# A hybrid encoder layer on one core: the order of loads at attention's opening, the place of the row maxima, and the step at which the output projection begins

## The chip, the cores and the metric

One core of a Trainium2 chip runs the whole program. The metric is the device time of one execution in microseconds; the figure for a kernel is the median of its runs. Engines are named as in the profile: PE is TensorE's matmul, PEld its weight load, ACT is ScalarE, DVE is VectorE, POOL is GpSimd, SP is SyncE, which here only issues DMAs.

## The reference, cut to what matters

One layer on 2048 tokens of width 1024, in float32:

```python
proj = jnp.einsum('btd,de->bte', x, w_in[l])
q, k, v, u, vs = jnp.split(proj, splits, axis=-1)     # 512 columns each
a_out = neighbourhood_attention(q, k, v, na_rel_bias[l])
s_out = spatial_gating(jax.nn.gelu(u), jax.nn.gelu(vs), ...)
mixed = jnp.concatenate([rms_norm(a_out, ...), rms_norm(s_out, ...)], axis=-1)
mix_out = jnp.einsum('bte,ed->btd', mixed, w_out[l])
x = layer_norm(DEEPNORM_ALPHA * x + mix_out, ln1_g[l], ln1_b[l])
moe_out = hierarchical_moe(x, ...)                    # 16 experts, two for each token
x = layer_norm(DEEPNORM_ALPHA * x + moe_out, ln2_g[l], ln2_b[l])
```

Attention has 8 heads of 64. The tokens form a grid of 32 rows of 64, and each attends to a window of 8 by 16 neighbours.

## The kernel before, in words

**Precision.** Each float32 factor is split into a high and a low part (`split`, line 142: ACT casts the high part, line 143; DVE subtracts it to give the low part, line 144), and each product is three matmuls (`passes`, lines 133 to 135). A "k step" of one 128-row block is thus three matmuls of up to 512 columns.

**Stage A, the input projection** (`phase_a`, line 147). Tokens come in two halves, columns in five groups of 512: Q (0), K (1), V (2), U (3), VS (4). One call of `block` does one column group of one half: two sets of four accumulators, and for each set eight k steps. While it runs, it loads the next group's eight weight pieces (`load_w`, 256 KB each: four at the first four k steps of either set). A piece goes through one of three raw buffers `wr`, is cast by ACT two turns later and finished by DVE. At the end of each set a `fin_...` function evicts the accumulators. For K (`fin_k`, line 362) that is an ACT cast and a DVE subtraction for each of the four, into staging tiles `mt` and `kt`, and four stores into the DRAM tensor `kd`.

The last call is `block(1, 1, ..., 2, then=attn_open(...))`: K of the second half, while the V weights are loaded. The V projection of that half isn't done in stage A. It is `late_v` (line 445), a generator over eight units of 128 tokens that does four k steps at each call; it serves as PE's filler in the first attention steps.

**Attention's opening** (`attn_open`, line 504) is a generator that `block` advances once for each k step of its second set. At its first call it closes the pools `sp` and `ev` and opens pool `ai` in their place, clears the `qb` and `lg` tiles on DVE, and loads K, Q and bias of group 0. The following calls load V block 0, then K, Q and bias of group 1, then V block 1, then the other two biases. A V block (`load_v`) is 256 tokens in four column pieces, each loaded by four DMAs of 48 or 64 KB: 16 DMAs.

**Attention** (`phase_b`, line 565). 128 steps, from a loop `for i in range(n + 5)`. Step i computes the scores of piece i (PE, three matmuls into a bank of tag `l`), adds the bias and takes the row maximum (DVE, line 644, into `lg` and `m`); it does the exponent of step i - 1 (ACT, line 651), the reciprocal of its sum (DVE, 656) and its scaling (POOL, 657); it transposes the probabilities of step i - 3 (PE, 670; ACT copies them into `pT`, 672). Odd steps mix steps i - 5 and i - 4 with V (PE, line 686). Tiles `m`, `s`, `pT` and the outputs of even groups come from pool `at`, which is opened on the same side as `ai` once stage A's pools are closed, and so takes over memory that stage A's staging tiles had; a tile waits for the last user of the memory that it gets.

What fills PE between scores: `late_v` in steps 0 to 13, nothing in steps 14 to PSTART - 1, then `project` (line 898), the output projection with 16 units of 128 tokens and eight turns each, one turn a step. A turn has six matmuls of 512 columns on average. After the loop the turns that are left run by themselves, with the first loads of the expert stage between them. Unit u needs the attention output of its 256 tokens; that of units 0 and 1 is complete after step 19. After a unit's last turn, `after` (line 719) does the layer norm and the routing in later turns: statistics, then POOL's root (line 728), then two DVE operations (730, 731), then PE's transposes of the normed rows (741), each a turn apart. In the loop, PSTART also places the first load of `sr` (step PSTART - 5), the first load of residual rows (PSTART) and four parameter loads (PSTART + 2). The split of the output weights (`load_wo`, lines 611 to 624) runs on ACT and DVE in steps 14 to 21.

**The expert stage** (`Moe`) follows: gathers, gate, up and down products of 16 experts with their weights streamed from HBM, and the last layer norm.

**Order.** PE, ACT, DVE and POOL run their instructions in the order in which the program issues them (line 1687 names these four); SP's order is left to the scheduler.

Of the kernel before, what the change touches and what calls it, by code (L numbers as in the profile page):

```python
# [8 lines left out]
F32 = mybir.dt.float32  # L9
# [8 lines left out]
P = 128  # L18
# [6 lines left out]
NCB = 4  # L25
# [14 lines left out]
LASTS = {max(j for j in range(len(JOBS) - 1) if JOBS[j][0] // 4 == g): g for g in range(4)}  # L40
NXG = 4
NVT = 12
PSTART = 21
LATE = 14
YB = 4
YG = 0
# [100 lines left out]
def phase_a(c, xT, w_in, wsT, bsT, sg_g, sg_b, tabM, tabE):  # L147
# [8 lines left out]
    with ExitStack() as es:  # L156
# [217 lines left out]
        def block(h, col, x, w, nxt, nxt_x=None, first=False, then=None):  # L374
            fin = {0: fin_q, 1: fin_k, 2: fin_v, 3: fin_u, 4: fin_vs}[col]
            wn, xn = [], []
            sets = ((0, 6), (6, 8)) if first else ((0, 4), (4, 8))
            for si, (a, b) in enumerate(sets):
                units = list(range(a, b))
                ps = [acc.tile([P, 512], F32, name="acc") for _ in units]  # L380
                for k in range(KC):
                    if first and si == 0:
                        if k + 1 < KC:
                            more = load_x(0, k + 1, x, 0)
                            load_w(2, k + 1, w, 0)
                            more()
                        pipe.step()
                    xh, xl = x[k]
                    wh, wl = w[k]
                    for i, u in enumerate(units):  # L390
                        if col >= 2:
                            s = slice(u * P, (u + 1) * P)
                            passes(nc, ps[i], xh[:, s], xl[:, s], wh, wl, k == 0, k == KC - 1)
                        else:
                            p, n = divmod(u, 2)
                            s = slice(n * 512, (n + 1) * 512)
                            m = slice(p * P, (p + 1) * P)
                            passes(nc, ps[i], wh[:, m], wl[:, m], xh[:, s], xl[:, s], k == 0, k == KC - 1)
                    if not (first and si == 0):
                        pipe.step()  # L400
                    if nxt is not None and k < 4:
                        if first and si == 0:
                            if k == 0:
                                pipe.add(load_sgu())
                        elif first:
                            load_w(nxt, k, wn)
                        elif si == 0:
                            load_w(nxt, k, wn)
                        else:
                            load_w(nxt, 4 + k, wn)  # L410
                    if first and si == 1 and k >= 4:
                        load_w(nxt, k, wn)
                    if nxt_x is not None and si == 1:
                        load_x(nxt_x, k, xn)()
                    if then is not None and si == 1:
                        next(then, None)
                g = fin(h, units, ps)
                if next(g) is not pipe:
                    pipe.add(g)
            return wn, xn  # L420
# [83 lines left out]
def attn_open(c, most, tabM, tabE):  # L504
    nc = c.nc
    most.close()
    c.at_es = ExitStack()
    at = pool(c, c.at_es, "ai", 2, "right")
    c.qb, c.lgs = qb, _ = [], []
    for i in range(2):  # L510
        q = at.tile([P, 2, NCB, P], F32R, name=f"qb{i}", bufs=1)
        nc.vector.memset(q[:, :, :, :].bitcast(F32), 0.0)
        qb.append(q)
    for i in range(4):
        l = at.tile([P, 12 * WIDE[i]], F32, name=f"lg{i}", bufs=1)
        nc.vector.memset(l, 0.0)
        c.lgs.append(l)

    vt, kt, tm = c.vt, c.kt, c.tm = {}, {}, {}

    def load_v(j, b):
        t = at.tile([P, 512], F32, name="vt", bufs=NVT)
        for r in range(4):
            o = r * 64 + COL0[b]
            nc.sync.dma_start(t[r * WIDE[b]:(r + 1) * WIDE[b]], c.vd[j][o:o + WIDE[b], :])
        vt[j, b] = t

    def load_kq(g):
        t, p = divmod(g, PAIRS)
        r0, R = quad_rows(t)  # L530
        k = at.tile([P, 2, 704], F32R, name="kt")
        nc.sync.dma_start(k[:, :, :R * 64].bitcast(F32), c.kd[p][:, :, r0 * 64:(r0 + R) * 64])
        kt[g] = k
        q = qb[g % 2]
        for h in range(2):
            s = slice(h * 64, h * 64 + 64)
            nc.sync.dma_start(q[s, :, :, s].bitcast(F32),
                              c.qd[p][s, t].rearrange("d l (b q) -> d l b q", b=NCB))

    def load_bias(t, p):  # L540
        tm[p] = at.tile([P, 11 * 80], F32, name=f"tm{p}", bufs=1)
        if t in (0, QUADS - 1):
            nc.sync.dma_start(tm[p][:, 0:8 * 80], tabE[t // (QUADS - 1), p])
        else:
            nc.sync.dma_start(tm[p], tabM[:, p])

    c.loads = load_v, load_kq, load_bias
    load_kq(0)
    load_bias(0, 0)
    yield  # L550
    for b in range(NCB):
        load_v(0, b)
    yield
    load_kq(1)
    load_bias(0, 1)
    yield
    for b in range(NCB):
        load_v(1, b)
    yield
    for p in range(2, PAIRS):  # L560
        load_bias(0, p)
        yield


def phase_b(c, x, w_out, mixg, ln1g, ln1b, w_r, b_r, m):
# [4 lines left out]
    with ExitStack() as es:  # L570
# [4 lines left out]
        load_v, load_kq, load_bias = c.loads  # L575
        at = pool(c, at_es, "at", 2, "right")
# [53 lines left out]
        def scores(i):  # L630
            g, b = divmod(i, NCB)
            t, p = divmod(g, PAIRS)
            r0, R = quad_rows(t)
            N = R * WIDE[b]
            at0 = R * (0, 24, 24, 56)[b]
            k4 = kt[g][:, :, :].rearrange("p l (r c) -> p l r c", c=64)
            rhs = [k4[:, l, 0:R, COL0[b]:COL0[b] + WIDE[b]] for l in range(2)]
            o = ps.tile([P, 512], F32, name="l")[:, 0:N].rearrange("p (r c) -> p r c", c=WIDE[b])
            passes(nc, o, qb[g % 2][:, 0, b], qb[g % 2][:, 1, b], rhs[0], rhs[1], True, True)
            bias = tm[p][:, at0:at0 + N]  # L640
            l = lgs[i % 4]
            m = at.tile([P, 1], F32, name="m", bufs=4)
            s = at.tile([P, 1], F32, name="s", bufs=4)
            nc.vector.tensor_tensor_reduce(out=l[:, :N], in0=o.rearrange("p r c -> p (r c)"), in1=bias, scale=-1.0,  # L644
                                           scalar=3.0e38, op0=OP.add, op1=OP.min, accum_out=m)
            work[i] = l, m, s
# [299 lines left out]
        for i in range(n + 5):  # L946
            if i == PRE:
                lazy.stage = pool(c, stage_es, "stage", NS, "right")
                for j in range(NS):
                    start(j, False)  # L950
            if i == LATE:
                c.held.close()
                open_late()
                fill = None
            if i < n:
                g, b = divmod(i, NCB)
                t, p = divmod(g, PAIRS)
                if b == 0 and 1 < g + 1 < QUADS * PAIRS:
                    load_kq(g + 1)
                if b == 0 and i and (i - 1) // 16 in (0, QUADS - 2):  # L960
                    load_bias((i - 1) // 16 + 1, (p - 1) % PAIRS)
            if i == LATE:
                pipe.add(load_wo())
            if 2 < i < 7:
                load_v(2, i - 3)
            if i < n:
                scores(i)
            if 0 <= i - 3 < n:
                flip(i - 3)
            if 0 <= i - 1 < n:  # L970
                expo(i - 1)
                norm(i - 1)
            if i % 2 and 0 <= i - 5 < n:
                mixv(i - 5)
                mixv(i - 4)
            if i == PSTART - 5:
                load_tok(0)
            if i == PSTART:
                load_res(0)
            if i == PSTART + 2:  # L980
                nc.sync.dma_start(lazy.lng, bcast(ln1g, D))
                nc.sync.dma_start(lazy.lnb, bcast(ln1b, D))
                nc.sync.dma_start(lazy.wr[:, :, 0:20], w_r)
                nc.sync.dma_start(lazy.br, bcast(b_r, 20))
            if i < LATE:
                next(fill)
            if i >= PSTART:
                if fill is None:
                    fill = project((i - PSTART) // 8)
                if next(fill) is pipe:  # L990
                    fill = None
            pipe.step()
        at_es.close()
        c.acc = "pp", "o"
        m.open(ps)
        u = -(-(n + 5 - PSTART) // 8)
        ahead = None
# [755 lines left out]
```

## Time and profile before

| | us |
|---|---|
| median of 3 runs | 1299.61 (1298.02 to 1303.31) |
| the profiled execution | 1294.98 |
| its span | 1293.2 |
| mean granted clock of PE in it | 0.977 |
| PE busy | 1211.4 |
| DVE, ACT, POOL busy | 741.6, 569.6, 402.6 |

The span runs from the first to the last instruction of the profiled execution. Start times in a timeline are microseconds from the start of the span. A bracket at the end of a line gives the idle time of the engine ahead of it and what ended it. The durations of matmuls overlap; the distance of two starts is what one costs. A granted clock of 1.00 is 2.4 GHz, half of it 1.2 GHz.

### The profile page before, as it was taken

To read this page: it belongs to the slowest core of one execution; us is meant where nothing else is said; L and a number is where in the kernel's file an instruction comes from. 1 tells how busy PE (TensorE), PEld (TensorE's weight loads), DVE (VectorE), ACT (ScalarE), POOL (GpSimd) and SP (SyncE) were. 2 spreads that over 40 slices of the span, in tenths; PEclk is the share of its full clock that TensorE was granted. 3 is DMA by queue.
4 is the path that set the end of the run, shared out by engine and by line. 5 is a ranking of instruction groups with operands and counts; after the bars stand their busy time and mean duration, and the time that the engine had idled before them with its cause. 6 is when DMAs were issued, how large, how long until landed. Compare 5 with 4: busy or idle time off the path is not lost. (4 is left out here: it accounts for less than half of the span.)

```text
span 1293.2 us, 22088 instructions
## 1 busy us (share of the span) xinstructions
PE 1211.4 (94%) x7900; PEld 1031.5 (80%) x7900; DVE 741.6 (57%) x1618; ACT 569.6 (44%) x1201; POOL 402.6 (31%) x420
## 2 busy tenths in 40 slices
PE   9999999999999898999999999888898999999980
PEld 7888888888888687887887887767787999998970
DVE  5466233435743226565765666766476578777665
ACT  4343142323332237554545544325466555555522
POOL 0011000001100013234344344443323356566475
PEclk9999999999999897999999999999999999999995
DMA  8514434450347769576686686455989899999984
GB/s 259 187 50 163 163 130 162 164 192 29 106 163 235 224 197 279 162 218 165 178 209 173 181 208 192 102 188 140 251 294 303 275 266 328 288 293 298 286 247 151
DMA packets 130913, 261.72 MB, mean 202 GB/s; under 512 B 52144, under 2 KB 53296, under 8 KB 130800
## 3 DMA queue, kind: packets, MB, share of 16 engines
q1 hardware_dynamic: 112816, 204.88, 50.6%
q0 software_dynamic: 17984, 55.40, 15.6%
q8 instruction: 63, 1.03, 0.3%
q14 instruction: 50, 0.41, 0.1%
HBM read 184.17 MB, written 80.24 MB: 204 GB/s over the span
## 5 line engine op out<-in xcount | busy, mean ns | idle before, releaser
L144 DVE TENSOR_TENSOR wl<-wr,wh 128x512 fp32r<-128x512 f32 (+1 forms) x132 | 125.5, 963 | 115.1 <-ACT wh L143 114.6
L657 POOL TENSOR_SCALAR lg<-lg,s 128x352 f32<-128x352 f32 (+3 forms) x128 | 76.0, 594 | 291.9 <-DVE s L656 222.6
L143 ACT CAST wh<-wr 128x512 fp32r<-128x512 f32 (+1 forms) x132 | 109.2, 840 | 90.8 <-DMA wr<-w_in 49.5
L133 PE MATMUL acc<-wh,xh 128*128 128x512 f32 x320 | 125.9, 393 | 0.0
L134 PE MATMUL acc<-wl,xh 128*128 128x512 f32 x320 | 125.0, 390 | 0.2 <-DVE wl L144 0.2
L135 PE MATMUL acc<-wh,xl 128*128 128x512 f32 x320 | 124.7, 390 | 0.2 <-DVE xl L144 0.2
L133 PE MATMUL gu<-xh,wh 128*128 128x256 f32 (+2 forms) x416 | 123.9, 298 | 0.0
L134 PE MATMUL gu<-xl,wh 128*128 128x256 f32 (+2 forms) x416 | 123.4, 297 | 0.0
L135 PE MATMUL gu<-xh,wl 128*128 128x256 f32 (+2 forms) x416 | 123.4, 297 | 0.0
L672 ACT COPY pT<-pt 128x384 f32<-128x384 f32 (+3 forms) x128 | 57.6, 450 | 116.6 <-PE pt L670 115.9
L133 PE MATMUL acc<-xh,wh 128*128 128x512 f32 x256 | 100.4, 392 | 0.0
L135 PE MATMUL acc<-xh,wl 128*128 128x512 f32 x256 | 99.7, 389 | 0.0
L134 PE MATMUL acc<-xl,wh 128*128 128x512 f32 x256 | 99.6, 389 | 0.0
L644 DVE CUSTOM_DVE_ANT_0 lg<-l,tm 128x352 f32<-128x352 f32 (+3 forms) x128 | 57.8, 452 | 65.1 <-PE l L135 41.3
L273 POOL TENSOR_TENSOR r<-va,mhalf 128x32 f32<-128x32 f32 x4 | 22.4, 5611 | 229.2 <-DVE va L271 229.2
L133 PEld LDWEIGHTS gu<-xh,wh 128*128 128x128 f32 x416 | 79.0, 190 | 1.4
L134 PEld LDWEIGHTS gu<-xl,wh 128*128 128x128 f32 x416 | 79.0, 190 | 1.1
L135 PEld LDWEIGHTS gu<-xh,wl 128*128 128x128 f32 x416 | 78.7, 189 | 0.0
L1257 POOL DMA_INDIRECT xad<-y,ix x33 | 56.4, 1709 | 49.4 <-ACT y L1236 29.8
L135 PEld LDWEIGHTS acc<-wh,xl 128*128 128x128 f32 x320 | 60.2, 188 | 13.3 <-DVE xl L144 0.7
L134 PEld LDWEIGHTS acc<-wl,xh 128*128 128x128 f32 x320 | 60.2, 188 | 13.0 <-DVE wl L144 1.0
L133 PEld LDWEIGHTS acc<-wh,xh 128*128 128x128 f32 x320 | 60.2, 188 | 12.3 <-ACT wh L143 0.3
(329 smaller groups left out, 3114.3 us busy)
## 6 DMA issues: line engine op xcount, KB each, us to landing
wr<-w_in SPq DMA_DIRECT2D x72, 256.0 KB
wr<-w_down SPq DMA_DIRECT2D x34, 512.0 KB
kt<-kd SPq DMA_DIRECT2D x24, 704.0 KB
wr<-w_gate SPq DMA_DIRECT2D x30, 512.0 KB
wr<-w_up SPq DMA_DIRECT2D x30, 512.0 KB
sd<-kt SPq DMA_DIRECT2D x16, 512.0 KB
qb<-qd SPq DMA_DIRECT2D x64, 128.0 KB
sr<-sd SPq DMA_DIRECT2D x16, 512.0 KB
```

The source lines that it names most:

```text
L133: nc.tensor.matmul(out, lhsT=ahi, rhs=bhi, start=first, stop=False)
L134: nc.tensor.matmul(out, lhsT=ahi, rhs=blo, start=False, stop=False)
L135: nc.tensor.matmul(out, lhsT=alo, rhs=bhi, start=False, stop=last)
L143: nc.scalar.copy(hi, src)
L144: nc.vector.tensor_tensor(lo, src, hi.bitcast(F32), op=OP.subtract)
L273: nc.gpsimd.tensor_tensor(r, va, mhalf[:, :, :], op=OP.pow)
L644: nc.vector.tensor_tensor_reduce(out=l[:, :N], in0=o.rearrange("p r c -> p (r c)"), in1=bias, scale=-1.0, scalar=3.0e38, op0=OP.add, op1=O ...
L657: nc.gpsimd.tensor_scalar(l[:, :N], l[:, :N], s, 1.0, op0=OP.mult, op1=OP.mult)
L672: nc.scalar.copy(w[0:n, 0:len(ch)], pt[0:n, 0:len(ch)])
L1257: return self.c.nc.gpsimd.indirect_dma_start(out=self.c.xad[0:rows, :], out_offset=bass.IndirectOffsetOnAxis(ap=ix, axis=0), in_=y, in_off ...
```

## The change

The output projection begins at step 20. The loader of attention is not called at k = 1 and 2, so its later parts come from k = 3 on, behind the loads of the V weights. V block 1 leaves the loader and is loaded in steps 0 and 1 of attention, two of its four pieces in each. The tiles `m` (row maxima) and `s` (row sums) come from pool `ai` in place of `at`.

```diff
-PSTART = 21
+PSTART = 20
...
-                    if then is not None and si == 1:
+                    if then is not None and si == 1 and k not in (1, 2):
                         next(then, None)
...
-    at = pool(c, c.at_es, "ai", 2, "right")
+    at = c.ai = pool(c, c.at_es, "ai", 2, "right")
...
     load_kq(1)
     load_bias(0, 1)
-    yield
-    for b in range(NCB):
-        load_v(1, b)
     yield
...
-            m = at.tile([P, 1], F32, name="m", bufs=4)
-            s = at.tile([P, 1], F32, name="s", bufs=4)
+            m = c.ai.tile([P, 1], F32, name="m", bufs=4)
+            s = c.ai.tile([P, 1], F32, name="s", bufs=4)
...
             if i == LATE:
                 pipe.add(load_wo())
+            if i < 2:
+                load_v(1, 2 * i)
+                load_v(1, 2 * i + 1)
             if 2 < i < 7:
                 load_v(2, i - 3)
```

## Rows read from the trace of the kernel before

**Rows 1.** The page: busy time of the engines; DMA share in 40 slices.

```profile
PE 1211.4 (94%) x7900; PEld 1031.5 (80%) x7900; DVE 741.6 (57%) x1618; ACT 569.6 (44%) x1201; POOL 402.6 (31%) x420
...
DMA  8514434450347769576686686455989899999984
```

**Rows 2.** Windows: stretch, length, busy time (instructions) by engine, clock, DMA share, GB/s.

```profile
420.60:444.77 24.17, 18.83 (x71) 14.43 (x69) 5.65 (x15) 5.37 (x11) 0.90 (x2) 0.86 0.72 229
444.77:483.00 38.23, 38.23 (x258) 31.85 (x257) 9.00 (x39) 13.46 (x44) 5.25 (x11) 1.00 0.69 204
490.00:500.00 10.00, 7.56 (x51) 5.47 (x51) 8.10 (x19) 9.03 (x21) 5.05 (x6) 0.54 0.94 289
```

**Rows 3.** Timeline of SP: start, duration, line, DMA, how many in a row.

```profile
407.61 9.55 SPq L525 DMA_DIRECT2D vt<-vd  x16
417.20 0.37 SPq L194 DMA_DIRECT2D wr<-w_in  x1
...
420.31 0.37 SPq L194 DMA_DIRECT2D wr<-w_in  x1
...
432.18 2.46 SPq L354 DMA_DIRECT2D kd<-kt  x2
```

**Rows 4.** Timelines of ACT and DVE at attention's opening.

```profile
426.14 0.62 ACT L143 CAST wh<-wr 128x512 fp32r<-128x512 f32 x1 [5.58 <-DMA wr<-w_in]
...
428.60 1.28 DVE L144 TENSOR_TENSOR kt<-acc,kt 128x512 fp32r<-128x512 f32 x2
439.78 0.36 DVE L644 CUSTOM_DVE_ANT_0 lg<-l,tm 128x192 f32<-128x192 f32 x1 [9.90 <-DMA kd<-kt]
```

**Rows 5.** Timeline of PE, from `late_v`'s first matmul to the first mixing with V.

```profile
420.59 0.39 PE L133 MATMUL pp<-wh,xh 128*128 128x512 f32 x1
...
424.67 0.39 PE L133 MATMUL pp<-wh,xh 128*128 128x512 f32 x1
...
426.81 0.50 PE L133 MATMUL pp<-wh,xh 128*128 128x512 f32 x1 [1.31 <-ACT wh L143]
...
429.34 0.44 PE L133 MATMUL l<-kt,qb 128*128 128x192 f32 x1 [1.06 <-DVE kt L144]
...
431.81 0.63 PE L134 MATMUL pp<-wl,xh 128*128 128x512 f32 x1
...
440.20 0.58 PE L133 MATMUL l<-kt,qb 128*128 128x256 f32 x1 [2.75 <-DVE m L644]
...
444.77 0.25 PE L133 MATMUL l<-kt,qb 128*128 128x192 f32 x1
...
448.07 0.25 PE L133 MATMUL l<-kt,qb 128*128 128x192 f32 x1
...
452.05 0.69 PE L686 MATMUL o<-pT,vt 96*64 96x64 f32 x16
```

**Rows 6.** Timelines of SP and PE where the output projection begins (steps 20 and 21).

```profile
494.41 0.43 SPq L892 DMA_DIRECT2D sr<-sd  x1
...
499.27 0.56 PE L133 MATMUL l<-kt,qb 128*128 128x264 f32 x1 [0.29 <-DVE s L656]
...
503.84 0.80 PE L133 MATMUL pp<-woh,sr 128*128 128x512 f32 x1
```

**Rows 7.** A later unit's norm on PE and DVE; PE's waits for it, 530 to 835.

```profile
598.64 0.32 PE L133 MATMUL l<-kt,qb 128*128 128x352 f32 x1
...
600.83 0.28 PE L133 MATMUL l<-kt,qb 128*128 128x264 f32 x1
...
600.88 1.27 DVE L730 SCALAR_TENSOR_TENSOR xt<-xt,mv,lng 128x1024 f32<-128x1024 f32 x1
603.64 1.59 DVE L731 SCALAR_TENSOR_TENSOR xt<-xt,r,lnb 128x1024 f32<-128x1024 f32 x1 [1.50 <-POOL r L728]
...
PE pt L741 <- DVE xt L731: 4.8, 5, 1.3
```

**Rows 8.** Windows: the turns of the projection behind attention's loop.

```profile
833.00:868.00 35.00, 30.24 (x171) 24.27 (x172) 23.35 (x58) 8.06 (x19) 14.45 (x13) 0.95 0.56 166
```

## The prediction, written before the changed kernel was run

> **What bounds the kernel now.** I read the page first: TensorE (PE) is busy 94% of the span and nothing else comes near [rows 1]. So time is won only where PE stands still, or runs at the lower clock. The windows by stretch show where that is around the change. In the stretch from the end of the last projection block to the scores of attention step 3, PE is busy 18.83 of 24.17 us at a granted clock of 0.86; in the next 38 us it never stops, at 1.00; from 490 to 500, around the step that the second edit concerns, it is at 0.54 [rows 2].
>
> The PE timeline names the stops of the first stretch [rows 5]. PE starts the late V projection (`late_v`) at 420.59, does seven of its eight k steps at 0.68 us each (six of them from 420.59 to 424.67), then waits 1.31 us for weight 7, then 1.06 us before the scores of step 0, then 2.75 us before those of step 2. Each stop is followed by matmuls at the lower clock of 1.2 GHz (one of 512 columns takes 0.63 us at 431.81, and they start 0.43 us apart).
>
> The SP timeline and those of ScalarE (ACT) and VectorE (DVE) say why [rows 3, 4]. Weights 6 and 7 are issued at 417.20 and 420.31, behind the 16 small loads of V block 0 that hold SP from 407.61 for 9.55 us. ACT waits 5.58 us for weight 7 and casts it at 426.14. Both engines work in order, so the evictions of the K block's accumulators stand behind that cast: the last ends at 429.88 (428.60 + 1.28). Their banks are those that the first scores write, which is the 1.06 us. The third stop is another kind: DVE's first softmax operation waits 9.90 us, until 439.78, for a store of K (`kd<-kt`). It doesn't read K. It writes the tile of row maxima, `m`, the first tile of pool `at`, which lies on memory that the staging tile of that store still holds.
>
> **The opening, part by part.** The change calls the loader of attention (`attn_open`) at k = 0 and then from k = 3 on, so the weights of k = 1 to 3 come ahead of the V pieces; it moves V block 1 (16 pieces) into steps 0 and 1; and it puts `m` and `s` in pool `ai`, whose memory was left by tiles used long before.
>
> Weight 7: issued at 420.31, its cast is read by PE at 426.81, and the three matmuls of its step are through at 428.28 (1.06 ahead of 429.34), so its other half was there by 427.8, 7.5 us after issue. PE wants it at 420.59 + 7 x 0.68 = 425.35. Were it issued at 417.20, where weight 6 is now, it would be ready at 424.7; ahead of all V pieces it is earlier still. So this stop goes even if part of the V pieces stay in front.
> The evictions: without the cast in front they start when the accumulators end, about 420.6. Now they take 3.1 us (from the end of the cast, 426.14 + 0.62, to 429.88), so 423.7; scores 0 want the banks at 420.59 + 8 x 0.68 = 426.03. Hidden, with 2 us to spare.
> The maxima: in `ai` nothing recent holds the memory. Nothing left to wait for.
> So scores 0 start at 426.03. Three steps follow at the pitch of an undisturbed one, 3.30 us (444.77 to 448.07 [rows 5]; it has two small transposes that steps 0 to 2 lack, which I leave in as margin), and scores 3 start at 435.9 in place of 444.77. **The opening gives 8.8 us**: 5.1 of named waits, the rest matmuls that no longer run at 1.2 GHz. The other end: if only the stop for `m` went, step 2 would last 3.30 in place of 4.57 us (440.20 to 444.77) and lose its 2.75 us wait: 4.0 us. More than 8.8 isn't there, since PE would then have no gap. I take 8.8.
>
> What now comes late? The 16 pieces of V block 1 cost SP some 9.55 us in another place, behind the stores of K and the first store of V. The K stores can be issued once evicted (423.7) and take 2.46 us for the last two, so 426.2, and land 5.1 us after (434.64 to 439.78 now [rows 3, 4]): 431.3. The pieces then run on SP to 435.8, and with the same 5.1 us the first eight are there at 436.1, all at 440.9. The first mixing with V comes 7.28 us behind scores 3 (452.05 against 444.77), so at 443.2, and the last eight are wanted two steps later. Hidden, by 7 us. What is queued behind them on SP is the store of V unit 1 and V block 2, which is wanted only from step 21 on. If that cover went, PE would wait in step 5.
>
> Here the Trainium skill speaks against the gain (DMA: Bandwidth & Descriptors, "Issuing engines are not separate DMA queues"). It says that all DMAs end up on the same 16 engines and interleave, and that the sequencer's time to start one is "usually small relative to the DMA itself". By that, the order on SP would hardly move the weights. The rows disagree: 16 small loads cost SP 9.55 us of issue, and weight 6 starts when they end [rows 3].
>
> **The earlier projection.** PSTART 20 lets the output projection start one step sooner. No PE work is added: six matmuls move from the end into step 20, and the loop behind attention has 15 turns in place of 16. At steps 20 and 21 PE already runs without a real wait (0.29 us at 499.27, then dense to the first projection matmul at 503.84 [rows 6]), at the lower clock. So what moves there fills nothing; it changes only which matmuls are slow. At the other end, PE idles 4.76 of 35.00 us over the 16 turns [rows 8], 0.3 us a turn: **0.3 us gained**. The loads that move with it: the first `sr`, issued at 494.41 for use at 503.84, is wanted at about 500.5 in the same frame, 6 us after issue where the K store above took 5.1. I cost it nothing; without that cover 1 to 2 us. The residual rows and the four parameter loads move a step too, on a queue that has gaps; nothing waits for them now.
>
> Every later step of the projection now falls on attention steps of the other parity (mixing with V comes in odd steps only). Its price isn't in the trace. Bounds: PE's transposes of the normed rows now wait five times for DVE, 4.8 us in all, where POOL's root came late (as before 603.64) [rows 7]: at best -4.8 us. At worst each of 14 projections waits the length of the mixing more, about 1.0 us (an estimate: 16 matmuls of it take 0.69 at 452.05, later steps have 24): +14. I take 0, since transposes come two steps behind the root before and after, one odd and one even step in both orders.
>
> **The sum**: -8.8 - 0.3 = -9.1 us. The profiled execution took 1294.98 (span 1293.2), so its like would take 1285.9. It lies 4.6 us under the median of the runs, 1299.61, and from that the forecast is 1290.5.
>
> **The rivals.**
> *The wait moves on* (0.14). `pT` is next in `at`, on the same memory, written first in step 3. If SP takes V block 1 ahead of the K stores, these land 9.55 us later, at 440.8, and ACT stands there for 4.9 us. Exponent, reciprocal and scaling behind it, some 2 us, bring the transposes of step 5 to 443, wanted at 442.5. With the other stops as a measure PE loses 1 us and 1 more at the lower clock. Gain 6.8 + 0.3: 1292.5. Against it: the K stores come first in the program.
> *The weights don't come sooner* (0.08). SP isn't among the engines whose order the program fixes (line 1687), so the pieces could still be put first. Then only `m`'s wait goes: 4.0 + 0.3, so 1295.3. The skill's rule above would give the same. Against it: weight 6 stands right behind the 16 pieces now, as the program has it.
> *Slower, by parity* (0.07). The place is the transposes of each projection, at the end of a step. The two DVE operations ahead of them take 1.27 and 1.59 us [rows 7]; an even step lasts 2.19 us (598.64 to 600.83). If the first starts at the end of an odd step, as it now starts at the end of an even one, 2.86 us of work meet a 2.19 us step, and with a root that is late as at 603.64 each projection waits some 1.0 us: +14 - 9.1 is 1304.5. It decides when the first of the two starts less than 0.7 us ahead of the step's end. Against it: it starts when the softmax operations of its step are through, and an odd step is longer behind that point.
> *Given back later* (0.06). The expert stage has its DMA engines busy nine tenths and more [rows 1]. If its weight stream set the end, the gain would be gone: 1299.6. Against it: that stream begins behind attention and moves with it.
> *Better* (0.05): the five waits go as well: 1285.7.
> The forecast itself has 0.60.
>
> **How the numbers follow.** 0.5% is 6.5 us, about what a measurement of this kernel can tell from no change; so faster means under 1293.1. The forecast with 3 us to each side lies below that for 0.52 of its 0.60; with the better case and 0.08 of the first rival that is 0.65. Slower than 1306.1 needs the parity rival beyond its price: 0.04. The rest, 0.31, is the same. The range of 1285 to 1298 holds the forecast with its spread, the better case and the first two rivals; it leaves out the slower one, the one given back and the edges, 0.16.
>
> **What would show it.** Right: weights 6 and 7 issued before the V pieces; no PE wait for `wh`, `wl`, `kt` or `m` between 420 and 436; a granted clock of 1.00 there; scores 3 some 15.3 us after the first matmul of `late_v` (24.2 now); the first mixing without a wait for a DMA. Wrong: a wait of ACT on `kd<-kt` at `pT`, a wait of PE for `vt` in step 5, waits at the transposes of every projection, or attention's later steps taking back what the opening gave.

## The result, and the profile after

The changed kernel takes **1316.47 us** (median of 4 runs, 1314.19 to 1317.03) against 1301.46 for the kernel before on the same chip (4 runs, 1298.02 to 1305.0). The ratio is 1.0117, its 95% interval 1.0091 to 1.0144: 15 us slower, where 9 us faster was forecast. The profiled execution took 1316.88 us (span 1315.1, mean granted clock 0.967); against the profiled execution of before, one of its faster ones, that is 21.9 us.

The page after, busy time of the engines and DMA share ([rows 1] before):

```profile
PE 1221.3 (93%) x7900; PEld 1041.0 (79%) x7900; DVE 747.5 (57%) x1618; ACT 570.1 (43%) x1201; POOL 398.9 (30%) x420
...
DMA  8514434541358778667688585454898899999974
```

As many instructions, no engine busier by more than 10 us; the page alone would not say where 22 us are. So I set the starts of the 128 attention steps (the first score matmul of each) of the two traces against each other, after minus before:

| step | 3 | 16 | 17 | 20 | 21 | 22 | 30 | 48 | 64 | 80 | 96 | 112 | 126 | 127 |
|---|---|---|---|---|---|---|---|---|---|---|---|---|---|---|
| us | -8.4 | -8.4 | -6.5 | -3.8 | -1.0 | -2.0 | -2.1 | -0.1 | +4.4 | +6.3 | +8.9 | +12.7 | +20.9 | +21.1 |

Three parts: the opening gives 8.4; steps 16 to 22 lose 6.4; steps 30 to 126 lose 23.0, with a recurrence every 16 steps. Behind attention 0.8 us more are lost (21.9 at the end).

**The opening.** Windows after, from 412 to the scores of step 3, then to 474, then around the projection's start (columns as in [rows 2]):

```profile
412.00:436.36 24.36, 24.36 (x113) 20.27 (x112) 6.10 (x15) 6.61 (x12) 0.90 (x2) 1.00 0.79 241
436.36:474.00 37.64, 37.64 (x256) 31.40 (x254) 8.94 (x38) 13.03 (x43) 5.24 (x11) 1.00 0.68 199
...
485.00:495.00 10.00, 5.29 (x37) 3.76 (x35) 7.97 (x19) 9.06 (x20) 4.60 (x5) 0.50 0.91 267
```

The SP timeline of the opening ([rows 3] before), and PE's first matmul of `late_v`, of scores 0 and of scores 3 ([rows 5] before):

```profile
409.19 1.10 SPq L194 DMA_DIRECT2D wr<-w_in  x2
410.35 8.01 SPq L525 DMA_DIRECT2D vt<-vd  x16
...
423.32 2.22 SPq L354 DMA_DIRECT2D kd<-kt  x2
...
428.25 10.98 SPq L525 DMA_DIRECT2D vt<-vd  x16
...
421.61 0.39 PE L133 MATMUL pp<-wh,xh 128*128 128x512 f32 x1
...
427.05 0.25 PE L133 MATMUL l<-kt,qb 128*128 128x192 f32 x1
...
436.36 0.25 PE L133 MATMUL l<-kt,qb 128*128 128x192 f32 x1
```

All weights go out ahead of the V pieces, PE never waits in the first 24 us, and its granted clock is 1.00 (2.4 GHz) there, where it was 0.86.

**Steps 16 to 22.** The SP timeline after ([rows 6] before), and PE's wait in step 20:

```profile
479.62 0.38 SPq L889 DMA_DIRECT2D sr<-sd  x1
482.94 2.90 SPq L607 DMA_DIRECT2D wo<-w_out  x2
485.93 0.55 SPq L532 DMA_DIRECT2D kt<-kd  x1
486.53 1.65 SPq L537 DMA_DIRECT2D qb<-qd  x2
...
495.52 0.56 PE L133 MATMUL l<-kt,qb 128*128 128x264 f32 x1 [3.09 <-DMA qb<-qd]
```

And SP before, at the same place:

```profile
487.20 0.56 SPq L532 DMA_DIRECT2D kt<-kd  x1
489.48 2.90 SPq L610 DMA_DIRECT2D wo<-w_out  x2
492.43 1.27 SPq L537 DMA_DIRECT2D qb<-qd  x2
```

The first `sr` (512 KB) goes out one step sooner, in the place that the K block of unit 5 had. The two loads of the output weights stand ahead of Q in both kernels; what is new is that K (704 KB) goes out behind them, straight ahead of Q. Q is in use 9.0 us after its first issue (486.53 to 495.52), where at most 6.8 us were enough before (492.43 to 499.27). So PE waits 3.09 us for it in step 20, and runs at 0.50 (1.2 GHz) in the 10 us from 485 to 495. Another 1.9 us go from step 16 to 17, where PE waits 3.30 us for DVE's maxima in place of 1.42; ACT had waited 1.77 us for the gains `mg`.

**Steps 30 to 126.** PE's waits from 465 to 835 after (columns: in all, how often, longest), and two lines of before for the same stretch, which had the 4.8 us for `xt` of [rows 7] and no wait for `sq`:

```profile
PE l L916 <- POOL sq L710: 9.2, 5, 2.7
PE l L133 <- ACT lt L749: 7.4, 5, 1.7
PE pt L738 <- DVE xt L728: 4.6, 6, 1.0
PE l L133 <- DVE m L641: 4.5, 2, 3.3
```

```profile
PE l L133 <- DVE m L644: 4.5, 3, 1.9
PE l L133 <- ACT lt L752: 1.9, 5, 0.4
```

New are `sq`, the wait of the sum-of-squares matmul for POOL's last add, and 5.5 us more for `lt`, the router's copy. These waits grow by 14.5 us (9.2 + 5.5 - 0.2). The windows from step 30 to step 126, before and after (columns as in [rows 2]), show the rest:

```profile
527.40:819.20 291.80, 282.34 (x2614) 236.02 (x2612) 187.34 (x634) 147.88 (x432) 113.01 (x162) 1.00 0.68 184
525.30:840.10 314.80, 291.16 (x2614) 241.73 (x2614) 193.75 (x644) 147.40 (x432) 115.99 (x165) 0.97 0.67 171
```

PE stands still for 23.6 us in place of 9.5, and the same 2614 matmuls keep it busy 8.8 us longer, at a granted clock of 0.97 in place of 1.00. The two make the 23.0. What POOL does ahead of one such add, before:

```profile
596.71 1.06 POOL L843 DMA_INDIRECT table<-xrec,ai  x1 [0.17 <-issue]
598.07 0.98 POOL L843 DMA_INDIRECT table<-xrec,ai  x1 [0.30 <-issue]
599.05 0.76 POOL L713 TENSOR_TENSOR sq<-sq,sp 128x256 f32<-128x256 f32 x1
599.76 0.50 POOL L657 TENSOR_SCALAR lg<-lg,s 128x264 f32<-128x264 f32 x1
600.43 1.07 POOL L843 DMA_INDIRECT gtok<-xrec,ai  x1 [0.17 <-issue]
601.81 1.19 POOL L843 DMA_INDIRECT gtok<-xrec,ai  x1 [0.31 <-issue]
603.00 0.60 POOL L728 TENSOR_TENSOR r<-mv,mhalf 128x1 f32<-128x1 f32 x1
...
602.46 0.61 PE L919 MATMUL l<-ones,sq 128*128 128x1 f32 x4
```

and after:

```profile
597.11 0.50 POOL L654 TENSOR_SCALAR lg<-lg,s 128x264 f32<-128x264 f32 x1
597.78 2.00 POOL L840 DMA_INDIRECT gtok<-xrec,ai  x1 [0.17 <-issue]
600.08 0.98 POOL L840 DMA_INDIRECT gtok<-xrec,ai  x1 [0.30 <-issue]
601.07 0.75 POOL L710 TENSOR_TENSOR sq<-sq,sp 128x256 f32<-128x256 f32 x1
601.75 0.58 POOL L725 TENSOR_TENSOR r<-mv,mhalf 128x1 f32<-128x1 f32 x1
...
597.58 1.27 DVE L727 SCALAR_TENSOR_TENSOR xt<-xt,mv,lng 128x1024 f32<-128x1024 f32 x1
...
601.88 0.61 PE L916 MATMUL l<-ones,sq 128*128 128x1 f32 x4 [2.23 <-POOL sq L710]
```

The routing (`route`) issues six indirect DMAs on POOL, each about 1 us of its queue. The add's place is fixed by attention's steps; the routing and the matmul that reads the sum follow the projection. Moving the projection by one step moved the last two issues (`gtok`) from behind the add to ahead of it, and the reader one step towards it. Before, the add ended at 599.81, 2.65 us ahead of its reader at 602.46. After, it ends 2.0 us later, at 601.82, and PE wanted it at 601.88 - 2.23 = 599.65, 2.8 us sooner. A margin of 2.65 became a lack of 2.2.

### The profile page after: what moved, and what is told of

Read it like the earlier page. It is cut to its first block, busy times and chain, and to the rows that moved or that the text cites. A ratio compares the mean times of both kernels' runs of the same rounds, so it can differ in the third digit from the quotient of the medians.

```text
span 1315.1 us, 22101 instructions
## 1 busy us (share of the span) xinstructions
PE 1221.3 (93%) x7900; PEld 1041.0 (79%) x7900; DVE 747.5 (57%) x1618; ACT 570.1 (43%) x1201; POOL 398.9 (30%) x420
## 5 line engine op out<-in xcount | busy, mean ns | idle before, releaser
L134 PEld LDWEIGHTS acc<-wl,xh 128*128 128x128 f32 x320 | 60.5, 189 | 12.5 <-DVE wl L144 0.4
```

The source lines that it names most:

```text
L134: nc.tensor.matmul(out, lhsT=ahi, rhs=blo, start=False, stop=False)
```

## The experiments

Times are medians; each ratio is against the kernel before on the same chip, with its 95% interval. "Lost in 30 to 126" is by how much a run's delay against the trace of before grows from step 30 to step 126.

| run | ratio | step 3 | step 22 | step 30 | step 126 | lost in 30 to 126 |
|---|---|---|---|---|---|---|
| changed kernel | 1.0117 | -8.4 | -2.0 | -2.1 | +20.9 | 23.0 |
| e1 | 0.9950 | -10.0 | -9.5 | -8.8 | -8.8 | 0.0 |
| e2 | 1.0296 | -1.4 | +4.6 | +4.6 | +42.7 | 38.1 |
| e3 | 0.9992 | -1.2 | -2.6 | -1.9 | -2.1 | -0.2 |
| e4 | 0.9970 | -3.2 | -4.0 | -3.9 | -3.8 | 0.0 |
| e5 | 0.9971 | -8.4 | -3.7 | -5.1 | -3.6 | 1.5 |
| e6 | 1.0261 | -9.9 | -1.7 | -1.7 | +37.7 | 39.4 |
| e7 | 1.0076 | -9.4 | -4.7 | -4.7 | +4.9 | 9.5 |
| e8 | 1.0196 | -8.0 | -5.2 | -5.1 | +31.3 | 36.5 |
| e9 | 1.0065 | -10.3 | -5.2 | -5.2 | +11.3 | 16.5 |
| e10 | 0.9937 | -9.6 | -8.9 | -8.3 | -4.6 | 3.7 |
| e11 | (other routing) | -9.7 | -7.5 | -7.5 | +14.7 | 22.1 |
| e12 | 1.0075 | -9.3 | -5.5 | -5.5 | +5.9 | 11.4 |

The column of step 3 also holds the moment at which `late_v` began, which differs by 2.2 us between these executions (419.76 in e9, 421.99 in e8). Counted from there, scores 3 come after 24.18 us before, 22.97 in e2 (whose opening is that of before), 23.11 in e3, 20.73 in e4, and 14.75 in each of the ten runs that have all edits of the opening.

### The parts one by one: e1, e2, e3, e4

e1 is the changed kernel without the earlier projection (the edit below); e2 is the kernel before with `PSTART` at 20 and nothing else:

```diff
-PSTART = 20
+PSTART = 21
```

> The changed kernel with PSTART back at 21: all of the opening's edits, the projection as before. Theory P (the earlier projection made the loss): scores of step 3 again 8.4 us earlier than before; of the 1.9 us that steps 16 to 17 lost to the late load of mg, all may stay, since SP's order up to there is that of the changed kernel; no further loss to step 127; so 6.5 to 8.4 us faster than before, about 1293 to 1295. Rival O (moving V block 1 into steps 0 and 1 upset SP's later order, and that made the loss): as slow as the changed kernel, 10 us or more over before.

Measured 1293.22 us, ratio 0.995 (0.9924 to 0.9976): faster than both kernels, as theory P had it.

> The kernel before with PSTART = 20 and nothing else. Theory P: opening as before; a wait for q of group 5 at step 20 (about 3 us, with a stretch at the lower clock some 4.5), since the first sr and two loads of output weights now stand ahead of it on SP; then some 23 us lost from step 30 to 127, in waits for sq, lt and xt that return every 16 steps; in all 20 to 28 us slower than before, about 1321 to 1329. Rival O: within 3 us of before.

Measured 1339.24 us, ratio 1.0296 (1.0241 to 1.0352). So the whole loss is the projection's, and alone it costs 40 us, where it costs 23 on top of the opening (e1 against the changed kernel). That was not expected; e8 and e11 show a part of the reason.

e3 is the kernel before with the loader's line alone, e4 with the tiles `m` and `s` alone:

```diff
-                    if then is not None and si == 1:
+                    if then is not None and si == 1 and k not in (1, 2):
```

> The kernel before with the loader not called at k = 1 and 2, V block 1 still in the loader, m and s still in pool at, PSTART 21. Theory: the waits of PE for weight 7 and for the evictions go, scores 0 start near 426, but the K stores still stand behind both V blocks on SP and land near 439.7, so the first softmax operation waits longer and step 2 starts where it did (440): nothing gained, 0 to -1 us. Rival, as the prediction had it (the two waits are separate gains): 4.8 us faster.

Measured 1298.15 us, ratio 0.9992 (0.9964 to 1.002): nothing gained, as expected.

```diff
-    at = pool(c, c.at_es, "ai", 2, "right")
+    at = c.ai = pool(c, c.at_es, "ai", 2, "right")
...
-            m = at.tile([P, 1], F32, name="m", bufs=4)
-            s = at.tile([P, 1], F32, name="s", bufs=4)
+            m = c.ai.tile([P, 1], F32, name="m", bufs=4)
+            s = c.ai.tile([P, 1], F32, name="s", bufs=4)
```

> The kernel before with only m and s moved to pool ai. Theory and prediction agree: the 9.9 us wait of DVE for the K store goes, the stops for weight 7 and the evictions stay, step 3 starts 4.0 us earlier and nothing else changes: 4 us faster, about 1297.5. If the wait goes to pT instead (same memory, first written in step 3, about 436 to 441), less than 2.

Measured 1296.47 us, ratio 0.997 (0.9947 to 0.9993), an interval that holds the 4 us that were expected. PE's only wait in e3's opening, scores 2:

```profile
438.90 0.58 PE L133 MATMUL l<-kt,qb 128*128 128x256 f32 x1 [6.65 <-DVE m L644]
```

With the weights early and the maxima still on the K stores' memory, what was won waits there: 6.65 us in place of the 2.75 of [rows 5]. Counted from `late_v`, e3 gains 1.1 us, no more than e2 with its unchanged opening, and e4 gains 3.5. Together they gain 9.4 (e1), more than the sum: the stops stand one behind the other, and each hid what the other was worth. e1 has the third edit too, V block 1 moved behind the K stores. No run has that edit by itself or leaves it out alone, so its share of the 9.4 us is not known.

### Is it the alignment, or the start? e5

The first projection still begins at step 20, but no projection work is issued in step 28, so that from step 29 on all stands as before:

```diff
-                if fill is None:
-                    fill = project((i - PSTART) // 8)
-                if next(fill) is pipe:
+                if fill is None and i != PSTART + 8:
+                    fill = project(max(0, i - 21) // 8)
+                if fill is not None and next(fill) is pipe:
                     fill = None
...
-        u = -(-(n + 5 - PSTART) // 8)
+        u = -(-(n + 5 - 21) // 8)
```

> The changed kernel, whose first projection still starts at step 20, but no projection work is issued in step 28, so from step 29 on every projection stands where it stood before the change. Theory (from step 30 on the loss comes from the alignment of projection, sum of squares and routing against attention's fixed order; the loads that move with the start cost only steps 16 to 21): steps 3 to 30 as in the changed kernel (8.4 us ahead of before at step 3, about 2 ahead at step 28), then no further loss: 1 to 3 us ahead of before at step 127, 1296 to 1300 us, and PE's waits for sq and lt back to those of before. Rival (the early loads at steps 16 to 21 put something out of step that stays, or the clock of TensorE stays lower after it): the loss of some 4 us per 16 steps goes on, 1312 to 1317.

Measured 1294.87 us, ratio 0.9971 (0.9945 to 0.9998). One empty turn brings back 21.5 us: steps 30 to 126 lose 1.5 in place of 23.0, and no wait for `sq` is left. The recurring loss is the alignment.

### Which wait carries it? e6, e7, e9

e6 puts the last add on DVE:

```diff
-                    nc.gpsimd.tensor_tensor(sq, sq, tmp, op=OP.add)
+                    (nc.vector if p == PAIRS - 1 else nc.gpsimd).tensor_tensor(sq, sq, tmp, op=OP.add)
```

> The changed kernel with the last of the four-pair sums of squares (the add of sp to sq at p = 3) on VectorE in place of GpSimd. Theory (the add stands on GpSimd's queue behind the indirect DMAs of the routing, and the sum-of-squares matmul, one step nearer to it than before, waits): PE's waits for sq, 9.2 us between 465 and 835, go, and with the matmuls at the lower clock behind them 10 to 14 us: 1302 to 1307 us; the waits for lt and xt stay. Rival (the whole GpSimd queue is late, not this add in it): the wait goes over to the root ra or to xt and lt, less than 4 us gained, 1312 or more. If VectorE is the tighter engine at that place, its softmax waits (m) grow by the 0.3 us of the add.

Measured 1333.78 us, ratio 1.0261 (1.0213 to 1.0309): a miss, and slower than the changed kernel. PE's longest sum of waits there, 465 to 835:

```profile
PE pt L738 <- DVE xt L728: 20.5, 11, 3.4
```

The wait for `sq` is gone, and the transposes wait 20.5 us in place of 4.6: the root `r`, next in POOL's queue behind the same issues, is late now. It is the queue that is late, as the rival said, not the add. By this, the lateness of the root was hidden behind the wait for `sq` in the changed kernel. Why e6 is slower still is shown in part: the first `gtok` issue of each routing lasts 1.93 to 2.06 us here (see e8).

e7 moves transposes, router and routing a turn later (`XW = 1` to `XW = 2`).

> The changed kernel with XW = 2: after the normed rows are stored, their transposes, the router's matmuls and the routing with its indirect DMAs come one turn later, which is the attention step at which they stood before the change; projection and sum of squares stay one step early. Theory (what costs is the routing's indirect DMAs and the router's matmuls against attention's fixed order): waits for lt and xt fall to a few us and the sq wait falls too, if the add now stands ahead of the DMAs: 1300 to 1306 us. Rival 1 (the sq wait comes from the norm and the add themselves, whatever the DMAs do): the sq wait of 9.2 us stays, lt and xt go, 1307 to 1312. Rival 2 (the lower clock, not the waits, is what costs): no more than 3 us gained.

Measured 1309.65 us, ratio 1.0076 (1.0044 to 1.0107); one of its eight executions took 6739 us, for a reason that is not known. The picture is its first rival's: `lt` falls to 1.9 us and the wait for `xt` goes, `sq` stays at 6.7, the maxima take 8.6 in place of 4.5, and 3.8 us of waits for DVE's `base` are new.

e9 leaves the routing where the change put it and issues the two `gtok` DMAs a turn later:

```diff
-                yield
+                for _ in range(1 + (j == 1)): yield
```

> The changed kernel with the last two of the routing's six indirect DMAs (those that write gtok) issued one turn later, so that on GpSimd the sum-of-squares add, the root r and the next scaling stand ahead of them. Theory (what holds the sum-of-squares matmul and the transposes is the pair of gtok issues in front of the add and the root, 2.3 to 3.3 us each time): the waits for sq, 9.2 us between 465 and 835, go, those for xt fall; the waits for lt, some 7 us, stay; of the 23 us that steps 30 to 127 lose 12 to 15 come back: 1301 to 1306 us. Rival (the add and the root are late for what feeds them, their own DVE and ACT producers one step closer): the sq wait only shrinks by a third or less, 1311 or more.

Measured 1306.61 us, ratio 1.0065 (1.0045 to 1.0086), just above the range that was expected. The wait for `sq` falls from 9.2 to 0.3 us, so the issues in front of the add were its cause. `lt` stays at 7.5; `xt` rises to 8.7, which was not expected, and only 6.5 of the 23.0 us come back in steps 30 to 126, where 12 to 15 were expected.

### The first load of sr: e8

```diff
-            if i == PSTART - 5:
+            if i == PSTART - 4:
                 load_tok(0)
```

> The changed kernel with the first load of sr at step 16 as before the change, so that SP takes kt and qb of group 5 ahead of it as before. Theory (steps 16 to 21 lose 7 us because sr and two wo loads are ahead of kt and qb of group 5 on SP): the wait for qb at step 20 goes, steps 19 to 21 lose 1 us or less in place of 5.5, and the end comes 4 to 5 us sooner, 1311 to 1313 us; the 1.9 us at step 16 stay, and so does the loss behind step 30. Rival: sr is then late for step 20 and PE waits there for it, 3 to 5 us, and nothing is gained: 1315 to 1318.

Measured 1326.97 us, ratio 1.0196 (1.0144 to 1.0248). The near part came as expected: K goes out ahead of the output weights again, PE's wait for Q in step 20 is gone, and steps 16 to 22 lose 2.4 us in place of 6.4. Q is there at most 6.5 us after its issue (487.73, used at 494.2 without a wait). But steps 30 to 126 lose 36.5, and the whole is 10 us slower than the changed kernel, which neither theory had. The routings tell a part of it. The first `gtok` issue of each of the five lasts 2.00, 1.98, 1.98, 1.66 and 1.90 us in e8; in the changed kernel it lasts 2.00, 1.05, 1.05, 1.95 and 1.90; in e2 all five last 1.75 to 1.99. One of them in e8, with the scaling ahead of it, the matmul that reads the sum, and DVE beside it:

```profile
648.13 0.48 POOL L654 TENSOR_SCALAR lg<-lg,s 128x264 f32<-128x264 f32 x1 [2.04 <-DVE s L653]
648.85 1.98 POOL L840 DMA_INDIRECT gtok<-xrec,ai  x1 [0.24 <-issue]
...
652.91 1.01 PE L916 MATMUL l<-ones,sq 128*128 128x1 f32 x4 [3.45 <-POOL sq L710]
...
648.64 1.27 DVE L727 SCALAR_TENSOR_TENSOR xt<-xt,mv,lng 128x1024 f32<-128x1024 f32 x1
```

and the same place in the changed kernel:

```profile
650.22 0.48 POOL L654 TENSOR_SCALAR lg<-lg,s 128x264 f32<-128x264 f32 x1
650.94 1.05 POOL L840 DMA_INDIRECT gtok<-xrec,ai  x1 [0.24 <-issue]
...
654.07 0.61 PE L916 MATMUL l<-ones,sq 128*128 128x1 f32 x4 [1.00 <-POOL sq L710]
...
651.01 1.27 DVE L727 SCALAR_TENSOR_TENSOR xt<-xt,mv,lng 128x1024 f32<-128x1024 f32 x1
```

In e8 the issue starts 0.21 us inside DVE's operation and ends 0.92 us behind it (650.83 against 649.91), about the 0.97 us that an issue takes by itself: it looks held until DVE is done. Started 0.07 us ahead of it, it takes 1.05.

### Does DVE hold the issue? e11

e8 with a copy on ACT in place of that operation of DVE, so that nothing with two inputs from SBUF runs there:

```diff
-            nc.vector.scalar_tensor_tensor(t, t, mv[:, 0:1], lazy.lng, op0=OP.subtract, op1=OP.mult)
+            nc.scalar.copy(t, t)
```

> The kernel of e8 (first state load later), in which each first gtok issue lasts 1.7 to 2.0 us and starts 0.2 to 0.5 us inside the first normalising operation of VectorE (xt<-xt,mv,lng, 1.27 us, two inputs from SBUF). Here that operation is left out: a copy on ScalarE stands in its place, so the mean isn't subtracted and the gain not applied. Theory (VectorE's operation with two SBUF inputs holds GpSimd's issue until it ends): the first gtok issues last 1.0 to 1.1 us, the add and the root behind them come 0.9 us sooner in each of five routings, the loss per 16 steps falls from 8 or 9 towards the 4 to 5 of the changed kernel: 1308 to 1318 us. Rival (the length comes from the DMA queue or the rows written, not from VectorE): 1.7 to 2.0 us as before, 1322 to 1332.

The whole took 1627.32 us and is not read: without mean and gain the tokens are routed otherwise and the expert stage is another. The attention steps stand ahead of it. The pair of the same routing:

```profile
643.39 1.04 POOL L840 DMA_INDIRECT gtok<-xrec,ai  x1 [0.23 <-issue]
644.74 0.97 POOL L840 DMA_INDIRECT gtok<-xrec,ai  x1 [0.30 <-issue]
...
646.52 0.61 PE L916 MATMUL l<-ones,sq 128*128 128x1 f32 x4 [2.52 <-POOL sq L710]
```

All five first issues last 1.04 or 1.05 us, the wait for `sq` falls from 16.8 to 12.5 us, and steps 30 to 126 lose 22.1 in place of 36.5. So DVE's operation did hold them, and the 4.3 us by which the wait for `sq` falls are what the five issues are shorter, 5.2 us in sum in place of 9.5. The rest of the 14.4 us can't be put down to the hold alone: with the operation off DVE, the transposes' wait for `xt` (4.7 us in e8) goes as well.

The hold is also only the smaller part of what e8 loses more than the changed kernel. PE waits 7.6 us more for `sq` there (16.8 against 9.2), but the five issues are only 1.6 us longer (9.5 against 8.0). The other 6.0 us are the place of the pair: in e8 it starts 0.2 to 1.5 us ahead of the moment at which PE wants the sum, in the changed kernel 1.3 to 2.1 us ahead. In the lines above it is 0.61 (648.85 against 652.91 - 3.45) and 2.13 us (650.94 against 654.07 - 1.00). e11, which holds no issue, has the places of e8, and still waits longer for `sq` than the changed kernel, in which three of five issues are held. e2 has these places and the held issues too. In e8 POOL's scaling ahead of the pair waits 2.04 us for DVE's `s`, in e11 2.10, in the changed kernel it doesn't wait. Why `s` comes later there isn't shown.

The Trainium skill (SBUF — State Buffer, "SBUF: two separate sides") says that of a VectorE instruction with two SBUF inputs and a GpSimd instruction that reads SBUF, the one that starts first has their shared ports to itself for the whole instruction, and the other is blocked fully. The trace agrees for the issue that came second (it ends 0.92 us behind DVE's end). It doesn't where the issue came first: DVE, 0.07 us behind it, still took its 1.27 us.

### Repaired versions: e12, e10

e12 joins e7 (for all units but the last two) and e9.

> The changed kernel with two repairs together: the transposes, router and routing one turn later (as in e7, but for all units except the last two), and the gtok pair one more turn later (as in e9). Projection still starts at step 20. Theory (the recurring loss of steps 30 to 127 is made of the sum-of-squares add and the root behind the routing's DMAs on GpSimd, and of the router's copy lt, and of nothing else): PE's waits for sq and for lt both at the level of the kernel before (none, and about 2 us), steps 30 to 127 lose 3 us or less in place of 23, and the time is 1296 to 1301 us. Rival (the repairs only move the wait, to the softmax maxima m or to the scaling, since attention's order has no free turn for it): 8 us or more are still lost there, 1303 to 1310.

Measured 1307.45 us, ratio 1.0075 (1.0056 to 1.0094): a miss, inside the range of its rival. Steps 30 to 126 lose 11.4 us, e7 alone lost 9.5: e9's line gives nothing more once the routing is moved. POOL ahead of an add in e12:

```profile
643.53 1.05 POOL L840 DMA_INDIRECT table<-xrec,ai  x1 [0.24 <-issue]
644.88 0.97 POOL L840 DMA_INDIRECT table<-xrec,ai  x1 [0.30 <-DVE xt L727]
645.87 0.74 POOL L710 TENSOR_TENSOR sq<-sq,sp 128x256 f32<-128x256 f32 x1
```

With the routing a turn later, the second pair of `table` issues stands where the `gtok` pair stood, and `sq` waits 6.6 us, as in e7 (6.7), where the same pair stands ahead of the add. Any pair there is enough, once its reader is a step nearer. `m` (8.1) and `base` (3.8) wait as in e7, too.

e10 is e1 with e9's line.

> The opening alone (projection from step 21 again) with the gtok pair one turn later. Theory: the root r no longer stands behind the pair, so the waits of PE's transposes for xt, about 5 us in the kernel before, shrink to 1 us or less: 3 to 6 us under the opening alone, 1287 to 1290.5 us, ratio 0.990 to 0.993. Rival: these waits are hidden by something else that is late next (the softmax operations on DVE behind the second normalising operation), and the time stays that of the opening alone, 1292 to 1295, ratio about 0.995.

Measured 1291.93 us, ratio 0.9937 (0.9915 to 0.9959), between theory and rival. The waits for `xt` are gone, but three waits for Q blocks, 5.7 us in all, take their place, at steps 60, 76 and 92. Why these loads come late there was not tried. It beats both kernels, and can't be told from e1.

## Why the prediction was wrong

**The opening was right, in mechanism and size.** From the first matmul of `late_v` to scores 3 were forecast 435.9 - 420.6 = 15.3 us; it is 14.75 (436.36 - 421.61), 24.2 before. The last K stores go out at 423.32 (forecast: 423.7). The 16 V pieces are through on SP at 439.23 (428.25 + 10.98; forecast: 435.8), and mixing still starts without a wait, at 443.63. Counted from `late_v` the 8.8 us became 9.4, since each of steps 0 to 2 takes 3.1 us where 3.30 was put in; at step 3 of this trace 8.4 are left, because `late_v` itself started 1.02 us later. The rivals of the opening fell: no wait at `pT`, and the weights do come sooner. The order on SP moves the weights as the rows said, though e3 shows that this alone is worth nothing at the end. The prediction also weighed a rule of the Trainium skill (DMA: Bandwidth & Descriptors, "Issuing engines are not separate DMA queues"), that the time to start a DMA is usually small relative to the DMA. It drew from it that the order would hardly matter. The trace doesn't bear that out: with the weights issued ahead of the V pieces PE waits for none, where it waited 1.31 us.

**The step that failed is "I take 0"** for the projection's new alignment, between -4.8 and +14. It was argued from one consumer, the transposes behind the root. Their waits stayed as they were, 4.6 us after and 4.8 before, but only behind the wait for `sq`: in e6, without it, they are 20.5, since the root stands behind the same issues. Never asked was which other pairs of producer and reader have one end tied to the attention steps and the other to the projection. Two show in the waits: `sq` (9.2 us from nothing) and `lt` (7.4 from 1.9). The routing's six issues on POOL, each of about 1 us, are not among what the prediction counts as moved. From the POOL lines of before shown above (596.71 to 603.00) the margin of 2.65 us for `sq` could have been read against a move of a whole step. The bound of +14 was too low as well: 23 us were lost, 14.2 of them with PE standing still and 8.8 in the same matmuls at a lower granted clock. The rival "Slower, by parity" had the right cause and sign in general but placed the wait at the transposes and gave it 0.07.

**The second failed term is the first `sr`**, at nothing, or 1 to 2 us without cover. I asked whether `sr` is in time, and it is. What stands behind it on SP is late: K of unit 5 lost its place to it, and Q behind K comes late. By e8 this costs 4.0 us (6.4 less 2.4), from one execution of each; the runs with the early `sr` lose 3.8 to 7.9 us in steps 16 to 22, e8 and e11 2.4 and 2.2.

**The 0.3 us** for one turn fewer behind attention is not to be found: 0.8 us are lost there, too little to tell from the differences between executions.

In attention nothing of the opening was given back after step 30: e1 keeps 8.8 us through step 126. Whether the expert stage gives some of it back can't be told. e1's profiled execution is behind by 1.1 us at the end, as e5's (by 3.2) and e10's (1.2) are, but the execution of before that they are set against was 4.6 us under its median; over many runs e1 gains 6 us (3 to 10 by its interval).

**Open** are the later place of the pair in e2, e6, e8 and e11, the wait for `xt` that e9 gained, the Q blocks of e10, and the 1.9 us from step 16 to 17. In e9 the root `r` starts inside DVE's first operation and takes 1.54 us in place of 0.58, which may be part of its wait for `xt`. e1 has that wait for the maxima too (3.29 us, step 17 at -8.1); from step 16 to 30 it loses 1.2 in all.

## What to carry to other kernels

Before moving one stream of work against another by a step, list each value that one stream makes and the other reads, and for each the margin in the trace: the end of the producer against the start of the reader. Then list what the moved stream issues on every queue, GpSimd's indirect DMAs included, and ask whom it now stands in front of. When stops stand one behind the other, try their repairs together: alone two of them gained 1.1 and 3.5 us here, all edits of the opening 9.4.

## What was not expected of the hardware

An indirect DMA's issue on GpSimd that takes 1.05 us takes up to 2.06 us (e6) when it starts inside a VectorE operation with two inputs from SBUF, and in e8 and the changed kernel it ends 0.92 to 0.94 us behind that operation; with the operation gone it takes 1.04 (e11). Started 0.07 us ahead of the operation, it takes 1.05 (changed kernel). Between e8 and e11 these held issues account for 4.3 us of PE's waits.
